# A decoder layer on one core: the product with w_out by Strassen's scheme, in seven half-size products

## The chip, the cores and the metric

One core of a Trainium2 chip. The metric is the device time of one execution in microseconds (us): the median of the runs.

## What is computed

The layer takes x (512 tokens, 1024 channels). One normalised copy of x goes through one wide input projection; two attention mixers, A and B, work on its pieces; their outputs are gated, widened to 1024 channels and merged. What matters here is the end:

```python
merged = g_m[..., :D_MODEL] * (y_a @ w_branch_a[l]) + g_m[..., D_MODEL:] * (y_b @ w_branch_b[l])
x = x + merged @ w_out[l]          # (512 x 1024) @ (1024 x 1024)
```

All of it is float32. The kernel computes each large product from three products of split operands: every float32 operand is cast to a high part (float32r) and a low part (the rest), and high times high, low times high and high times low are added up in PSUM.

## The kernel before

The whole kernel is one Python function, hybrid_kernel, that writes out five engine queues by hand. Generators for the attention (attention), the projections (gemms) and the compression (cmp) yield the cost of each piece of TensorE work; a loop at its end takes the pieces in turn and keeps a planned time. Everything that is not TensorE work is queued as a Chain: a list of steps with costs per engine, taken from a heap in order of planned time. A step with two costs (the helper either) goes to VectorE or to GpSimd, whichever the plan says ends first. So the order on each engine is fixed when the kernel is built; on the chip each engine goes through its own queue in that order and waits at semaphores.

Weights come through Stream (W): load issues a DMA of a tile (128 x 512, 256 KB) into one of four raw buffers, split casts it to the high part wh on ScalarE or GpSimd (L295, L297) and subtracts for the low part wl on VectorE or GpSimd (L299), and take hands four, two or one of them to a product. Every DMA goes through the helper dma (L212) on the SyncE queue.

The part that the change touches is the end of gemms. For each of the two mixers and each of the eight tiles j of 128 channels, gmgate makes a gate (24 matmuls of 512 columns into pgc; L1161 scales it on VectorE) and branch makes the widened mixer output (12 matmuls of 512 columns into pbr; L1179 multiplies it by the gate). With the second mixer the two are added (L1236) and the sum, 128 channels x 512 tokens, is cast to mh (L1237, ScalarE) and ml (L1238). Then comes the output product: for each of four groups of 256 output columns and each of four tiles of 128 tokens, 8 x 3 matmuls of 256 columns into a PSUM tile po, one VectorE instruction that adds 0.25 times the result to the tile xr of x (L1264), and a DMA of 128 KB to out_y. The 16 weight tiles of w_out go through the same Stream as all others; each is split once. The loads of x are issued during the last two tiles and the first columns of the output.

Of the kernel before, what the change touches and what calls it, by code (L numbers as in the profile page):

```python
# [18 lines left out]
S = 512  # L19
# [67 lines left out]
def hybrid_kernel(ctx: ExitStack, tc: tile.TileContext, x, x0, xT, wtok, wchan, gains, w1,  # L87
# [14 lines left out]
    def nm(s):  # L102
# [11 lines left out]
    ap_ = ctx.enter_context(tc.tile_pool(name="att", bufs=NATT))  # L114
    sp = ctx.enter_context(tc.tile_pool(name="sp", bufs=2))
    RES = {"g": (pg, 2), "s": (pss, 2), "t": (pst, 3), "o": (pso, 1), "sb": (sp, 3), "gmt": (sp, 3), "nraw": (sp, 4),
           "ph": (sp, 3), "P": (sp, 2), "p0": (sp, 2), "T": (sp, 2), "pf": (sp, 2)}
    held = {k: [] for k in RES}
    waiters = {k: [] for k in RES}
    owner, keep = {}, []  # L120
# [145 lines left out]
        return f  # L266


    class Stream:


        def __init__(w, tiles, bufs, hi, lo):
            w.tiles, w.bufs, w.mk_hi, w.mk_lo = tiles, bufs, hi, lo
            w.raw, w.out, w.chain, w.i, w.loaded = {}, {}, {}, 0, 0

        def load(w):
            i = w.loaded
            if i < len(w.tiles) and i - len(w.chain) < w.bufs:
                src, n = w.tiles[i]
                t = wp.tile([P, WT], F32, name=nm("wr"), tag="wraw", bufs=NRAW)[:, :n]  # L280
                w.raw[i] = t, dma(t, src, 4 * n)
                w.loaded += 1

        def split(w, upto):
            for i in range(len(w.chain), min(upto, len(w.tiles))):
                while w.loaded <= i:
                    w.load()
                n = w.tiles[i][1]
# [12 lines left out]

        def take(w, n, width):

            w.split(w.i + n)
            r = []
            for i in range(w.i, w.i + n):
                hi, lo = w.out.pop(i)
                r += [(hi[:, k:k + width], lo[:, k:k + width], w.chain[i])
                      for k in range(0, w.tiles[i][1], width)]
            w.i += n  # L310
            return r

# [160 lines left out]
    tiles = []  # L473
    for n_ in ORDER_T:
        tiles += tok_tiles(n_) if n_ in tlay else chan_tiles(n_)
    for w in range(2):
        for j in range(8):
            tiles += chan_tiles(f"gm{8 * w + j}") + [(wbr[j, w], 512)]
    for c in range(4):
        tiles += [(wout[c, i], 512) for i in range(4)]  # L480
    W = Stream(tiles, NRAW - 1, lambda: wp.tile([P, WT], F32R, name=nm("wh"), tag="whi"),
               lambda: wp.tile([P, WT], F32R, name=nm("wl"), tag="wlo"))
    W1 = Stream([(w1[kv, q], 512) for kv in range(2) for q in range(8)], 1, lambda: att("vh"), lambda: att("vl"))

    def ahead(f):

        W.split(W.i + min(4, int(f * 4 + 0.8)))

    def gemm_tok(name, emit, tags="gggg"):
        n = tlay[name][2]  # L490
# [325 lines left out]
    class Unit:  # L816
# [103 lines left out]
        def pv(u, kb):  # L920
            z, ch = u.p[kb]
            yield ch.ready
            ws = z["w"]
            if kb == 0 and u.first:
                yield room("o")
                O[0] = psum("o", "O")
            n = S - kb * P
            for i, w in enumerate(ws):
                v = u.v()[kb]
                nc.tensor.matmul(O[0][:, S - n:], v.bitcast(F32) if kb == 3 else v, w,  # L930
                                 start=(u.first and kb == 0 and i == 0), stop=(u.last and kb == 3 and not u.before))
# [265 lines left out]
    def gemms():  # L1197
# [19 lines left out]
        yield from zgate("b", 1)  # L1217
        yield from zgate("b", 2)
        yield from zgate("b", 3)
        xr = {}  # L1220
        ms = []
        for j in range(8):
            yield from gmgate(0, j)
            yield from branch(0, j)
        for j in range(8):
            yield from gmgate(1, j)
            if j == 6:
                for t in range(0, NT, 2):
                    yield room("P")
                    xp = alloc("P", "xr", (P, 1280))  # L1230
                    for i in range(2):
                        xr[t + i, 0] = xp[:, i * 512:(i + 1) * 512]
                        dma(xr[t + i, 0], x[(t + i) * P:(t + i + 1) * P, :512], 2048)
            ch = yield from branch(1, j)
            g0, g1, a, b = gms[0, j][0], gms[1, j][0], att("mh"), att("ml")
            ch.do(either(512), lambda e, g0=g0, g1=g1: e.tensor_add(g0, g0, g1))  # L1236
            ch.do({"A": ca(512)}, lambda e, g0=g0, a=a: e.copy(a, g0))  # L1237
            ch.do(either(512), lambda e, g0=g0, a=a, b=b: e.tensor_sub(b, g0, a.bitcast(F32)))  # L1238
            ms.append((a, b, ch))
        for c in range(4):  # L1240
            ws = W.take(4, 256)
            if c == 0:
                for t in range(NT):
                    xr[t, 1] = att("xr", F32)
                    dma(xr[t, 1], x[t * P:(t + 1) * P, 512:], 2048)
            st = [[(a[:, t * P:(t + 1) * P], b[:, t * P:(t + 1) * P], ch) for a, b, ch in ms] for t in range(NT)]
            pss_ = {}
            for t in range(NT):
                if c == 0 and t == 0:

                    for i in range(2):
                        yield room("g")
                        pss_[i] = psum("g", "po")
                        yield from mm3(pss_[i][:, :256], st[i][:7], ws[:7], stop=False)
                if t in pss_:
                    yield from mm3(pss_[t][:, :256], st[t][7:], ws[7:], start=False)
                    ps = pss_[t]
                else:
                    yield room("g")
                    ps = psum("g", "po")  # L1260
                    yield from mm3(ps[:, :256], st[t], ws)
                ahead((t + 1) / NT)
                xv = xr[t, c // 2][:, (c % 2) * 256:(c % 2 + 1) * 256]
                ch = Chain(now[0] + 230).do({"D": 335}, lambda e, xv=xv, ps=ps: e.scalar_tensor_tensor(  # L1264
                    xv, ps[:, :256], 0.25, xv, op0=ALU.mult, op1=ALU.add), ps)
                ch.call(lambda t=t, c=c, xv=xv: dma(out[t * P:(t + 1) * P, c * 256:(c + 1) * 256], xv, 1024))

    def cmp():
        yield from compress_h(0)
# [63 lines left out]
def _layout(inp):  # L1333
# [4 lines left out]
    for name, cols in tok_pieces().items():  # L1338
# [13 lines left out]
    wo = f["w_out"][0].reshape(4, 2, P, 4, 256).transpose(3, 0, 2, 1, 4).reshape(4, 4, P, 512)  # L1352
# [28 lines left out]
```

## Time and profile before

| | |
|---|---|
| median of 3 runs | 476.97 us (476.38 to 478.19) |
| the profiled execution | 477.26 us |
| its span, first to last instruction | 475.1 us |
| TensorE clock granted | 1.0 of full speed |
| instructions | 8579 |
| bytes moved | 49.18 MB, mean 104 GB/s |

In the rows below PE is TensorE, PEld its weight loads, DVE is VectorE, ACT ScalarE, POOL GpSimd, SP SyncE and SPq its DMA queue. A start is in us from the start of the span. A duration includes the way through the engine, so instructions of one engine that follow each other start closer together than their durations say: what counts for a queue is the distance from start to start. The time of the profiled execution is 2.16 us longer than its span, and 0.29 us over the median.

### The profile page before, as it was taken

Reading aid. Unit: us, or ns where it says so; the run is one execution under the profiler, and the core shown is the slowest. Engines: PE = TensorE matmul, PEld = TensorE weight load, DVE = VectorE, ACT = ScalarE, POOL = GpSimd, SP = SyncE. Lnnn points to the kernel's source line nnn. Section 1 sums busy time; section 2 is a strip of 40 time slices with the busy share of each in tenths; the row PEclk is TensorE's granted clock in tenths of the full one; section 3 lists DMA queues with packets and bytes.
Section 4 is the critical chain, followed back from the end, with each engine's and each line's share of the span. In section 5 each row is a group of like instructions: output and inputs, shape, how many; then the busy total and the mean of one; then the engine's idle time right before and its main releaser. Section 6 shows DMA issues by size and latency. Waiting matters only on the chain.

```text
span 475.1 us, 8579 instructions
## 1 busy us (share of the span) xinstructions
PE 467.9 (98%) x3020; PEld 421.6 (89%) x3020; DVE 336.3 (71%) x843; ACT 252.9 (53%) x603; POOL 167.5 (35%) x230
## 2 busy tenths in 40 slices
PE   9999989999999999999999999999999999999997
PEld 8999789999999989888888888888888888889997
DVE  5877999599999499977877786868734556464331
ACT  7666586588775275576776446677522222132210
POOL 0455486136663064256453324745520010000000
PEclk9999999999999999999999999999999999999999
DMA  8844244443335123032212322212122324554421
GB/s 294 243 131 112 66 112 123 144 137 117 112 110 149 52 74 105 24 88 68 67 46 66 90 90 68 66 46 67 68 66 89 111 68 118 168 187 121 140 89 46
DMA packets 27899, 49.18 MB, mean 104 GB/s; under 512 B 3088, under 2 KB 5520, under 8 KB 27856
## 3 DMA queue, kind: packets, MB, share of 16 engines
q1 hardware_dynamic: 27856, 48.63, 34.1%
q8 instruction: 24, 0.39, 0.3%
q14 instruction: 19, 0.16, 0.1%
HBM read 45.87 MB, written 2.75 MB: 102 GB/s over the span
## 4 chain that ended last, share of the span: by engine, by line
PE 87%; DVE 7%; issue 2%; ACT 2%; DMA 1%; POOL 1%; SPq 0%; DVEq 0%; POOLq 0%
PE pgc L324 28%; PE pgt L324 18%; PE po L324 10%; PE pbr L324 9%; PE O L930 6%; PE pt L896 6%; PE sps L849 3%; PE sps L850 3%; DVE wl L299 2%; PE pq L793 1%; DVE qs L801 1%; DMA x<-in_xT 1%; PE hps L687 1%; PE hps L686 1%; DVE X L658 1%
## 5 line engine op out<-in xcount | busy, mean ns | idle before, releaser
L299 DVE TENSOR_TENSOR wl<-wr,wh 128x512 fp32r<-128x512 f32 (+1 forms) x111 | 80.0, 723 | 9.1 <-ACT wh L295 8.5
L324 PE MATMUL pgc<-hh,wh 128*128 128x512 f32 x208 | 84.0, 404 | 0.0
L324 PE MATMUL pgt<-wh,hh 128*128 128x256 f32 (+1 forms) x288 | 82.6, 287 | 0.6 <-ACT nraw L552 0.6
L324 PE MATMUL pgt<-wl,hh 128*128 128x256 f32 (+1 forms) x288 | 81.6, 283 | 1.2 <-DVE wl L299 0.7
L324 PE MATMUL pgc<-hh,wl 128*128 128x512 f32 x208 | 82.1, 395 | 0.0
L324 PE MATMUL pgc<-hl,wh 128*128 128x512 f32 x208 | 82.0, 394 | 0.0
L324 PE MATMUL pgt<-wh,hl 128*128 128x256 f32 (+1 forms) x288 | 81.1, 282 | 0.0
L295 ACT CAST wh<-wr 128x512 fp32r<-128x512 f32 (+1 forms) x85 | 51.1, 615 | 23.9 <-DMA wr<-in_wout 21.5
L868 DVE CUSTOM_DVE_ANT_0 sb<-sps,T 128x512 f32<-128x512 f32 (+3 forms) x96 | 46.3, 486 | 22.9 <-PE sps L850 21.9
L883 ACT ACTIVATE P<-sb,sst 128x512 f32<-128x512 f32 (+3 forms) x88 | 50.9, 580 | 13.3 <-DVE sst L868 12.4
L887 POOL TENSOR_SCALAR P<-P,sst,gate 128x512 f32<-128x512 f32 (+3 forms) x56 | 38.5, 692 | 50.5 <-DVE sst L886 45.8
L324 PEld LDWEIGHTS pgt<-wl,hh 128*128 128x128 f32 x288 | 54.2, 188 | 1.8 <-DVE wl L299 1.1
L324 PEld LDWEIGHTS pgt<-wh,hh 128*128 128x128 f32 x288 | 54.3, 188 | 1.4 <-ACT nraw L552 0.8
L324 PEld LDWEIGHTS pgt<-wh,hl 128*128 128x128 f32 x288 | 54.3, 189 | 0.3
L297 POOL TENSOR_SCALAR wh<-wr 128x512 fp32r<-128x512 f32 (+1 forms) x39 | 25.8, 665 | 71.0 <-DMA wr<-in_wchan 48.2
L908 ACT CAST ph<-pt 128x512 fp32r<-128x512 f32 (+2 forms) x72 | 33.2, 479 | 30.1 <-PE pt L896 29.4
L324 PEld LDWEIGHTS pgc<-hl,wh 128*128 128x128 f32 x208 | 39.1, 188 | 9.1
L324 PEld LDWEIGHTS pgc<-hh,wh 128*128 128x128 f32 x208 | 39.2, 188 | 7.4
L324 PEld LDWEIGHTS pgc<-hh,wl 128*128 128x128 f32 x208 | 39.2, 188 | 7.2
L365 POOL TENSOR_TENSOR nr<-nss,mhalf 128x4 f32<-128x4 f32 x28 | 30.8, 1102 | 33.6 <-DVE nss L364 26.9
L896 PE MATMUL pt<-cst,P 128*128 128x128 f32 x232 | 40.6, 272 | 0.6 <-POOL P L887 0.6
L910 DVE TENSOR_TENSOR pl<-pt,ph 128x512 fp32r<-128x512 f32 (+2 forms) x72 | 38.2, 549 | 3.2 <-ACT ph L908 3.2
(202 smaller groups left out, 1062.4 us busy)
## 6 DMA issues: line engine op xcount, KB each, us to landing
wr<-in_wchan SPq DMA_DIRECT2D x52, 256.0 KB, 2.7
wr<-in_wtok SPq DMA_DIRECT2D x36, 256.0 KB, 2.8
T<-rtab SPq DMA_DIRECT2D x16, 256.0 KB, 3.8
wr<-in_w SPq DMA_DIRECT2D x16, 256.0 KB, 2.7
wr<-in_wbr SPq DMA_DIRECT2D x16, 256.0 KB, 2.6
wr<-in_wout SPq DMA_DIRECT2D x16, 256.0 KB, 3.1
xr<-in_x SPq DMA_DIRECT2D x8, 256.0 KB, 3.9
out_y<-xr SPq DMA_DIRECT2D x16, 128.0 KB, 1.7
```

The lines of the kernel that those rows point to most:

```text
L295: e.copy(hi, raw)
L297: e.tensor_scalar(hi, raw, 1.0, 1.0, op0=ALU.mult, op1=ALU.mult)
L299: c.do(either(n), lambda e, hi=hi, lo=lo, raw=raw: e.tensor_sub(lo, raw, hi.bitcast(F32))).mark((w, 1, i))
L324: nc.tensor.matmul(dst, sts[i][a], mvs[i][b], start=(start and i == a == b == 0), stop=(stop and i == n - 1 and b == 1))
L365: c.do({"p": 430 + 150 * w}, lambda e: e.tensor_tensor(v(dst), v(ss), mhalf[:parts, :w], op=ALU.pow))
L868: e.tensor_tensor_reduce(z["sb"][:, :L], sps[:, :L], T[:, S - L:], scale=-1.0, scalar=3e38, op0=ALU.add, op1=ALU.min, accum_out=st[:, 0, b ...
L883: e.activation(pv(), z["sb"][:, :L], AF.Exp, bias=st[:, 0, b:b + 1], scale=-1.0, accum_out=st[:, 1, b:b + 1])
L887: c.do({"P": 315 + 0.834 * L}, lambda e: e.tensor_scalar(pv(), pv(), st[:, 2, b:b + 1], g, op0=ALU.mult, op1=ALU.mult))
L896: nc.tensor.transpose(pt[:, (b - kb) * P:(b - kb + 1) * P], u.p0 if u.p0 is not None and b == 0 else u.pb[:, POFF[b] + kb * P:POFF[b] + (k ...
L908: e.copy(z["w"][0], pt[:, :w])
L910: ch.do({"D": cd(w)}, lambda e: e.tensor_sub(z["w"][1], pt[:, :w], z["w"][0].bitcast(F32)), pt)
L930: nc.tensor.matmul(O[0][:, S - n:], v.bitcast(F32) if kb == 3 else v, w, start=(u.first and kb == 0 and i == 0), stop=(u.last and kb == 3 ...
```

## The change

The output product is cut into blocks: A is the merged input, A11 its tokens 0 to 255 in channels 0 to 511, A12 the same tokens in channels 512 to 1023, A21 and A22 the other tokens; B is w_out cut in the same way. Seven products of 256 x 512 by 512 x 512 take the place of eight:

| product | left factor | right factor | goes to |
|---|---|---|---|
| 1 | A11 | B11 | all four blocks of the output |
| 2 | A12 | B21 | block 11 |
| 3 | S4 = A12 - S2 | B22 | block 12 |
| 4 | A22 | B21 - T2 | block 21 |
| 5 | S1 = A21 + A22 | T1 = B12 - B11 | blocks 12 and 22 |
| 6 | S2 = S1 - A11 | T2 = B22 - T1 | blocks 12, 21 and 22 |
| 7 | S3 = A11 - A21 | B22 - B12 | blocks 21 and 22 |

Each product is 2 tiles of tokens x 4 tiles of channels x 3 matmuls of 512 columns; the last tile of product 4 is made in two halves of 256 columns. A tile leaves PSUM when it is done. Products 1 and 7 are moved up: product 1 stands between gmgate and branch of the second mixer's tile 4, product 7 between those of its tile 6 (EARLY). Products 5 and 6 come first after tile 7, in two passes (three tiles of channels of both, then the fourth), and then 2, 3 and 4.

The left factors are made in merged by VectorE or GpSimd from the merged tiles and split like before. The right factors are objects of the class Sum: their sources are loaded by load_sums in 36 DMAs of 256 KB (B11 twice, B12 twice, B22 three times, B21 twice, 4 tiles each) in place of 16, into the pool ph, which held the transposed attention weights; it has six buffers now, and the low parts pl of those come from it too. VectorE or GpSimd subtracts where two sources make a factor. The four tiles of T1 and T2 are kept in wsum. Where product 1 leaves PSUM, ScalarE copies it times 0.25 to a tile u, VectorE adds it to one output tile, and GpSimd adds u to three others.

```diff
+EARLY = {4: 1, 6: 7}
+PACE = 800
...
-           "ph": (sp, 3), "P": (sp, 2), "p0": (sp, 2), "T": (sp, 2), "pf": (sp, 2)}
+           "ph": (sp, 6), "P": (sp, 2), "p0": (sp, 2), "T": (sp, 2), "pf": (sp, 2)}
...
+    (b11, b12), (b21, b22) = [[[wout[i, j, k] for k in range(4)] for j in range(2)] for i in range(2)]
+    t1 = [Sum(z, k, True, None, True) for k, z in enumerate(zip(b12, b11))]
+    t2 = [Sum((b22[k],), k, True, t1[k]) for k in range(4)]
+    right = {1: [Sum((z,), home=True) for z in b11], 7: [Sum(z) for z in zip(b22, b12)], 5: t1, 6: t2, 2: [Sum((z,)) for z in b21],
+             3: [Sum((z,)) for z in b22], 4: [Sum((b21[k],), k, False, t2[k]) for k in range(4)]}
...
         for j in range(8):
             yield from gmgate(1, j)
-            if j == 6:
+            if j == 0:
...
+                W.load_sums()
...
+            if j == 2:
...
+                for t, c in ((0, 0), (1, 0), (2, 0), (3, 0), (2, 1), (3, 1), (0, 1), (1, 1)):
+                    dma(xr[t, c], x[t * P:(t + 1) * P, c * 512:(c + 1) * 512], 2048)
+            if j in EARLY:
+                yield from early[EARLY[j]]()
             ch = yield from branch(1, j)
...
+        if j < 4:
+            q = att("ms", F32)
+            sub(c, q[:, lo_], m[:, lo_], m[:, hi_])
+            part(c, a[:, lo_], b[:, lo_], m[:, lo_])
+            part(c, a[:, hi_], b[:, hi_], q[:, lo_])
...
+        c.do(either(256), lambda e: e.tensor_add(q[:, hi_], n[:, hi_], m[:, hi_]))
+        c.call(lambda: d.start(c.t))
+        sub(c, n[:, lo_], q[:, hi_], n[:, lo_])
+        sub(c, n[:, hi_], m[:, lo_], n[:, lo_])
+        c.call(lambda: f.start(c.t))
+        part(d, u, v, q[:, hi_])
+        part(c, x, y, n)
+        part(f, a, b, m)
...
+            u = att("u", F32)
+            z[1].do({"A": 478}, lambda e: e.activation(u, z[0], AF.Copy, scale=0.25))
+            add(z, t, 0, 0, True)
+            for r, col in ((1, 0), (1, 1), (0, 1)):
+                add(z, t, r, col, src=u)
...
+        yield from products((S1, "tt", five), (S2, "ss", six))
+        for left, tags, r, col in ((A12, "gg", 0, 0), (S4, "to", 0, 1), (A22, "sst", 1, 0)):
```

The order of all engines is the same as before up to the second mixer's tile 0. Two places behind it matter below. The first is VectorE around the second mixer's tiles 5 to 7. Before, a tile j is the scaling of the gate (L1161), two or three low parts of weights (wl, L299), the product with pbr (L1179), the sum (L1236) and its low part (L1238); the rows begin behind the scaling of tile 6:

```order
L299 TENSOR_TENSOR wl_5585<-wr_5537,wh_5584 128x512
L299 TENSOR_TENSOR wl_5592<-wr_5544,wh_5591 128x512
L1179 SCALAR_TENSOR_TENSOR gm_5531<-gm_5531,pbr_5575 128x512
L299 TENSOR_TENSOR wl_5599<-wr_5550,wh_5598 128x512
L1236 TENSOR_TENSOR gm_4981<-gm_4981,gm_5531 128x512
L1238 TENSOR_TENSOR ml_5601<-gm_4981,mh_5600 128x512
L1161 TENSOR_TENSOR gm_5602<-pgc_5603,R 128x512
```

Now (wq and wl of L348 are the sources and low parts of product 7's right factor, ms, s1l, sl and ml parts of the left factors, gm_5681 the gate of tile 6):

```order
L348 TENSOR_TENSOR wl_5670<-wq_5195,wh_5669 128x512
L1341 TENSOR_TENSOR gm_4719<-gm_4719,gm_5608 128x512
L1359 TENSOR_TENSOR sl_5607<-gm_3831,sh_5606 128x512
L348 TENSOR_TENSOR wl_5676<-wq_5265,wh_5675 128x512
L1378 TENSOR_TENSOR ms_5314<-gm_3961,gm_4719 128x256
L1355 TENSOR_TENSOR gm_3961<-ms_5314,gm_3961 128x256
L1359 TENSOR_TENSOR s1l_5605<-ms_5314,s1h_5604 128x256
L1355 TENSOR_TENSOR gm_3961<-gm_4719,gm_3961 128x256
L1250 TENSOR_TENSOR gm_5681<-pgc_5682,R 128x512
L348 TENSOR_TENSOR wl_5728<-wq_5328,wh_5727 128x512
L348 TENSOR_TENSOR wl_5726<-wq_5307,wh_5725 128x512
```

The low parts of product 7's third and fourth weight tile (wl_5726, wl_5728) stand behind the scaling of tile 6's gate, which needs the whole of pgc_5682; on TensorE the matmuls of product 7 follow pgc_5682 at once.

The second place is SyncE's queue of DMAs. Before, the loads for the second mixer's tiles 5 to 7 are these, three to a tile:

```order
L212 DMA wr_5407<-in_wchan 128x512
L212 DMA wr_5414<-in_wbr 128x512
L212 DMA wr_5420<-in_wchan 128x512
L212 DMA wr_5472<-in_wchan 128x512
L212 DMA wr_5479<-in_wbr 128x512
L212 DMA wr_5485<-in_wchan 128x512
```

Now, ahead of wr_5422, the second weight tile of the gate of tile 4:

```order
L214 DMA wr_5345<-in_wchan 128x512
L214 DMA wq_5351<-in_wout 128x512
L214 DMA wq_5360<-in_wout 128x512
L214 DMA xr_5363<-in_x 128x512 x2
L214 DMA xr_5364<-in_x 128x512 x2
L214 DMA xr_5367<-in_x 128x512
L214 DMA xr_5368<-in_x 128x512
L214 DMA xr_5365<-in_x 128x512
L214 DMA xr_5366<-in_x 128x512
L214 DMA wq_5403<-in_wout 128x512
L214 DMA wr_5422<-in_wchan 128x512
L214 DMA wr_5427<-in_wbr 128x512
```

All eight loads of x and three of w_out now stand between two loads of gate weights that used to follow each other; six more loads (four wq from in_wout and two wr) stand just ahead of the first of these rows.

## Rows read from the trace of the kernel before

**Rows 1.** The page's busy time of each engine over the span, and its 40 slices of the span (busy tenths; PEclk is the granted clock in tenths).

```profile
PE 467.9 (98%) x3020; PEld 421.6 (89%) x3020; DVE 336.3 (71%) x843; ACT 252.9 (53%) x603; POOL 167.5 (35%) x230
...
PE   9999989999999999999999999999999999999997
...
DVE  5877999599999499977877786868734556464331
...
POOL 0455486136663064256453324745520010000000
PEclk9999999999999999999999999999999999999999
```

**Rows 2.** The chain that ended last, in order of time, from the second mixer's tile 0 to the end: start, us, what, count. A piece of TensorE work begins here where the one before it ended.

```profile
359.30 5.55 PE pgc L324 x24
364.86 2.80 PE pbr L324 x12
...
392.73 5.54 PE pgc L324 x24
398.27 2.79 PE pbr L324 x12
...
423.33 2.78 PE pbr L324 x12
426.10 5.37 PE po L324 x45
431.48 0.02 issue
431.50 0.44 DVE xr L1264
431.94 0.04 issue
431.98 40.01 PE po L324 x336
471.99 0.02 issue
472.01 0.42 DVE xr L1264
```

**Rows 3.** Busy time of each engine in stretches: one tile of the second mixer (gate and branch) and two stretches of the output product. Columns: stretch, its length, then PE, PEld, DVE, ACT, POOL busy us (instructions), granted clock, DMA share, GB/s.

```profile
401.06:409.39 8.33, 8.33 (x38) 6.77 (x37) 4.57 (x7) 2.28 (x4) 0.62 (x1) 1.00 0.30 91
...
437.50:448.90 11.40, 11.40 (x99) 11.40 (x98) 4.09 (x8) 2.48 (x4) 0.00 (x0) 1.00 0.48 144
448.90:460.40 11.50, 11.50 (x100) 11.50 (x99) 4.09 (x8) 1.86 (x3) 0.00 (x0) 1.00 0.35 109
```

**Rows 4.** VectorE in order of time in the second mixer's tile 0, and at the first output tiles: start, us, instruction, and in brackets how long the engine stood idle before it and for whom.

```profile
364.89 0.69 DVE L1161 TENSOR_TENSOR gm<-pgc,R 128x512 f32<-128x512 f32 x1 [4.26 <-PE pgc L324]
...
367.69 0.69 DVE L1179 SCALAR_TENSOR_TENSOR gm<-gm,pbr 128x512 f32<-128x512 f32 x1 [0.20 <-PE pbr L324]
368.29 0.68 DVE L299 TENSOR_TENSOR wl<-wr,wh 128x512 fp32r<-128x512 f32 x1
368.89 0.68 DVE L1236 TENSOR_TENSOR gm<-gm,gm 128x512 f32<-128x512 f32 x1
370.27 0.69 DVE L1238 TENSOR_TENSOR ml<-gm,mh 128x512 fp32r<-128x512 f32 x1 [0.69 <-ACT mh L1237]
...
431.50 0.77 DVE L1264 SCALAR_TENSOR_TENSOR xr<-po,xr 128x256 f32<-128x256 f32 x2 [2.08 <-PE po L324]
```

**Rows 5.** GpSimd's groups of instructions over the span, shapes kept apart: count, busy us, mean ns of one, idle time before.

```profile
L297 POOL TENSOR_SCALAR wh<-wr 128x512 fp32r<-128x512 f32 x38 | 25.2, 665 | 71.0 <-DMA wr<-in_wchan 48.2 <-DMA wr<-in_wout 11.0 <-DMA wr<-in_wtok 6.3
L299 POOL TENSOR_TENSOR wl<-wr,wh 128x512 fp32r<-128x512 f32 x13 | 18.2, 1398 | 24.1 <-ACT wh L295 23.4
...
L564 POOL TENSOR_TENSOR nxn<-nraw,nr 128x256 f32<-128x256 f32 x6 | 4.0, 668 | 0.3
```

**Rows 6.** VectorE and GpSimd side by side, in order of time, at two moments (sps and O are PSUM tiles, wr and wh lie in SBUF).

```profile
54.67 1.31 POOL L299 TENSOR_TENSOR wl<-wr,wh 128x512 fp32r<-128x512 f32 x1
54.91 1.62 DVE L299 TENSOR_TENSOR wl<-wr,wh 128x512 fp32r<-128x512 f32 x1
...
203.57 1.29 POOL L299 TENSOR_TENSOR wl<-wr,wh 128x512 fp32r<-128x512 f32 x1
203.74 0.69 DVE L868 CUSTOM_DVE_ANT_0 sb<-sps,T 128x512 f32<-128x512 f32 x1 [1.33 <-PE sps L850]
204.36 0.68 DVE L959 TENSOR_TENSOR ys<-O,ot 64x512 f32<-64x512 f32 x1
```

**Rows 7.** The same view as rows 3, for three stretches in which the DMA queue was full; the last column is what it moved.

```profile
5.00:10.00 5.00, 4.88 (x35) 4.33 (x36) 4.06 (x7) 4.54 (x9) 0.62 (x1) 1.00 1.01 376
10.00:15.00 5.00, 5.00 (x44) 5.00 (x44) 5.00 (x9) 4.99 (x10) 1.31 (x1) 1.00 1.06 337
...
412.00:414.00 2.00, 2.00 (x10) 1.61 (x9) 0.69 (x1) 0.00 (x0) 0.00 (x0) 1.00 0.88 237
```

**Rows 8.** The end, in order of time: the last matmul, the last VectorE instruction and the issue of the last DMA.

```profile
471.70 0.28 PE L324 MATMUL po<-wl,mh 128*128 128x256 f32 x1
472.01 0.42 DVE L1264 SCALAR_TENSOR_TENSOR xr<-po,xr 128x256 f32<-128x256 f32 x1 [2.40 <-PE po L324]
472.47 0.33 SPq L212 DMA_DIRECT2D out_y<-xr  x1
```

More of the change, by code (lines that the diff above doesn't have):

```diff
@@ L266, in all_of, with __init__, dst, fire @@
         return f
+    class Sum:
+        def __init__(z, srcs, keep=None, put=False, prior=None, home=False):
+            z.srcs, z.keep, z.put, z.prior, z.home = srcs, keep, put, prior, home
+            z.raw, z.t, z.c, z.left, z.next = [], 0.0, Chain(held=True), 1, None
+            if prior:
+                z.left += 1
+                prior.next = z
+            if len(srcs) == 2:
+                z.c.do(either(512), lambda e: e.tensor_sub(z.dst(), z.raw[0], z.raw[1]), lambda: z.raw[1])
+            elif keep is not None:
+                z.c.do(either(512), lambda e: e.tensor_sub(z.dst(), z.raw[0], wsum[keep]))
+            if put:
+                z.c.call(lambda: release(z.raw[0], z.c.t))
+        def dst(z):
+            return wsum[z.keep] if z.put else z.raw[0]
+        def fire(z, t):
+            z.t = max(z.t, t)
+            z.left -= 1
+            if not z.left:
+                z.c.start(max(now[0], z.t))
+        def end(z):
+            if not z.put:
+                release(z.raw[0], z.c.t)
+            if z.next:
+                z.next.fire(z.c.t)
+    wsum = []
     class Stream:
@@ L273, in __init__ @@
             w.tiles, w.bufs, w.mk_hi, w.mk_lo = tiles, bufs, hi, lo
-            w.raw, w.out, w.chain, w.i, w.loaded = {}, {}, {}, 0, 0
+            w.raw, w.out, w.chain, w.i, w.loaded, w.ahead, w.next = {}, {}, {}, 0, 0, 0, 0
         def load(w):
+            while w.loaded < len(w.tiles) and isinstance(w.tiles[w.loaded], Sum):
+                w.loaded += 1
             i = w.loaded
-            if i < len(w.tiles) and i - len(w.chain) < w.bufs:
+            if i < len(w.tiles) and w.ahead < w.bufs:
                 src, n = w.tiles[i]
@@ L308, in take @@
                 r += [(hi[:, k:k + width], lo[:, k:k + width], w.chain[i])
-                      for k in range(0, w.tiles[i][1], width)]
+                      for k in range(0, hi.shape[-1], width)]
             w.i += n
@@ L485, in ahead @@
     def ahead(f):
-        W.split(W.i + min(4, int(f * 4 + 0.8)))
+        n, k = 0, min(4, int(f * 4 + 0.8))
+        while k and W.i + n < len(tiles):
+            k -= not getattr(tiles[W.i + n], "home", False)
+            n += 1
+        W.split(W.i + n)
     def gemm_tok(name, emit, tags="gggg"):
@@ L1232, in gemms @@
                         xr[t + i, 0] = xp[:, i * 512:(i + 1) * 512]
[L1233 removed]
+                for t in range(NT):
+                    tag = "sb" if t < 2 else "T"
+                    yield room(tag)
+                    xr[t, 1] = alloc(tag, "xr")
+                for t, c in ((0, 0), (1, 0), (2, 0), (3, 0), (2, 1), (3, 1), (0, 1), (1, 1)):
+                    dma(xr[t, c], x[t * P:(t + 1) * P, c * 512:(c + 1) * 512], 2048)
@@ L1240, in gemms @@
[L1240 to L1266, printed above, removed]
@@ new lines, in hybrid_kernel, with products @@
+    one = []
+    xr = {}
+    pend = {}
+    def products(*todo):
+        ws = [W.take(4, 512) for _ in todo]
+        ps, n = {}, 0
+        m = 3 if len(todo) > 1 else 4
+        for k in (0, 3) if m == 3 else (0,):
+            e = 4 if k else m
+            for i, (left, tags, f) in enumerate(todo):
+                for t, tag in enumerate(tags):
+                    o = slice((t - 1) * 256, t * 256) if t and len(tags) > 2 else slice(0, 512)
+                    t = min(t, 1)
+                    st = [(a[:, t * P:(t + 1) * P], b[:, t * P:(t + 1) * P], c) for a, b, c in left[k:e]]
+                    if not k:
+                        yield room(tag)
+                        ps[i, t, o.start] = psum(tag, "po")
+                    p = ps[i, t, o.start]
+                    for v in mm3(p[:, o], st, [(h[:, o], l[:, o], c) for h, l, c in ws[i][k:e]], start=not k, stop=e == 4):
+                        yield v
+                        if not callable(v):
+                            n += 1
+                            ahead(n / 8 / len(todo))
+                    if e == 4:
+                        f(t, (p, Chain(now[0] + 230)), o)
@@ new lines, in add @@
+    def add(z, t, r, col, frees=False, o=slice(0, 512), src=None):
+        p, c = z
+        key = 2 * r + t, col
+        dst = xr[key]
+        pend[key] = pend.get(key, 0) + 1
+        if src is None:
+            c.do({"D": cd(o.stop - o.start)}, lambda e: e.scalar_tensor_tensor(
+                dst[:, o], p[:, o], 0.25, dst[:, o], op0=ALU.mult, op1=ALU.add), p if frees else None)
+        else:
+            c.do({"P": cg(512)}, lambda e: e.tensor_add(dst, dst, src))
+        c.call(lambda: pend.__setitem__(key, pend[key] - 1))
@@ new lines, in send, with f, out1 @@
+    def send(z, t, r, col, o=slice(0, 512)):
+        key = 2 * r + t, col
+        def f():
+            assert pend[key] == (o.stop < 512 and not z[2:])
+            dma(out[key[0] * P:(key[0] + 1) * P, col * 512 + o.start:col * 512 + o.stop], xr[key][:, o],
+                4 * (o.stop - o.start))
+        z[1].call(f)
+    def out1():
+        def f(t, z, _):
+            u = att("u", F32)
[3 more added lines that the diff above has]
+                add(z, t, r, col, src=u)
+        yield from products((A11, "tt", f))
@@ new lines, in out7, with f, output, five @@
+    def out7():
+        def f(t, z, _):
+            add(z, t, 1, 0)
+            add(z, t, 1, 1, True)
+        yield from products((S3, "ss", f))
+        i = tiles.index(right[5][0])
+        for k in range(4):
+            Chain(now[0] + PACE * k).call(lambda k=k: W.split_sum(i + k))
+    early = {1: out1, 7: out7}
+    def output():
+        def five(t, z, _):
+            add(z, t, 1, 1)
+            add(z, t, 0, 1, True)
+        def six(t, z, _):
+            add(z, t, 1, 1)
+            send(z, t, 1, 1)
+            add(z, t, 0, 1)
+            add(z, t, 1, 0, True)
+        yield from products((S1, "tt", five), (S2, "ss", six))
+        for left, tags, r, col in ((A12, "gg", 0, 0), (S4, "to", 0, 1), (A22, "sst", 1, 0)):
+            def f(t, z, o):
+                for q in (slice(0, 256), slice(256, 512)):
+                    if o.start <= q.start < o.stop:
+                        y = z if o.stop - o.start > 256 else (*z, 1)
+                        add(z, t, r, col, q.stop == o.stop, q)
+                        send(y, t, r, col, q)
+            yield from products((left, tags, f))
```

98 lines of the change are left out of this document (85 added, 13 removed).

## The prediction, made before the changed kernel ran

> **What bounds the kernel now.** I read the busy times and slices first: TensorE is busy 98% of the span at the full clock in every slice, VectorE 71%, and in the last tenth VectorE is half idle and GpSimd idle altogether [rows 1]. Next the chain that ended last: from 359.30 to 471.99 it is matmuls end to end, apart from one turn of VectorE at 431.50, and the output product takes 426.10 to 471.99, 45.89 us [rows 2]. So what counts is how many matmuls this stretch has, how long each takes, and whether their inputs stay ahead. Then the stretches: a tile of the second mixer leaves VectorE 4.57 us busy of 8.33 and GpSimd 0.62; the output product leaves VectorE 4.09 of 11.4 and GpSimd nothing [rows 3]. The change spends that idle time. The end is one VectorE turn and one DMA after the last matmul [rows 8].
>
> **TensorE, the gain.** Before: 384 matmuls of 256 columns; 336 of them took 40.01 us, 0.119 each [rows 2]. A matmul of 512 columns: from 359.30 to 426.10 there are 8 tiles of 36, 288 matmuls in 66.80 us, 0.232 each [rows 2]. The change issues 7 x 24 = 168 matmuls of 512 columns, but 12 of them as 24 halves: 156 x 0.232 = 36.2 and 24 x 0.119 = 2.9, together 39.0, and 0.16 for the last matmul's way out (0.28 against 0.12 from start to start [rows 8]): 39.2. That is 6.7 less than 45.89. The widths alone give little (two of 256 against one of 512 is 0.238 to 0.232); the eighth product gives the rest.
>
> **The end.** The last piece is again 256 columns wide, read by one VectorE instruction and sent as 128 KB, as at 472.01 and 472.47 [rows 8]: no difference. Moving products 1 and 7 up costs TensorE nothing in itself, as one accumulator follows another without a gap today [rows 2].
>
> **VectorE and GpSimd, the price.** VectorE has 55 instructions more, GpSimd 18. A 512-wide VectorE instruction starts 0.60 after the one before it, a 256-wide one takes 0.35 (0.77 for two, less the way out) [rows 4]. On GpSimd a 512-wide copy takes 0.62 to 0.67, a two-input instruction 1.3 alone (mean 1.4), a 256-wide one 0.67 [rows 5, 6]. The two also get in each other's way: a VectorE subtraction that began 0.24 after GpSimd's took 1.62 in place of 0.68 and ended 0.55 after GpSimd's end, while two VectorE instructions that read PSUM kept 0.69 and 0.68 beside the same kind of GpSimd work [rows 6]. So VectorE's SBUF-to-SBUF work and GpSimd's work add up, and the reading of PSUM lies beside.
>
> The place where this binds first is product 7. Without stalls the gate of tile 4 ends at 398.27 [rows 2], product 1 at 403.84, its first half at 401.05, branch 4 at 406.62, the gate and branch of tile 5 at 412.19 and 414.97, the gate of tile 6 at 420.53, and there product 7 begins. Its third weight tile's low part is read by the ninth matmul, issued at 420.53 + 8 x 0.232 - 0.16 = 422.2. VectorE makes that low part (wl_5726) as the 26th instruction counted from the first read of product 1, and only two behind the scaling of tile 6's gate, which can't start before 420.53 + 0.03 (364.86 to 364.89 [rows 2, 4]).
>
> - From below: three starts of 0.60 from 420.56, and 0.08 for the way out, is 422.44. Product 7 waits 0.2 at least, however idle VectorE was before.
> - From above: of the 26, 19 are wide and 7 narrow, 13.9 us. GpSimd has in the same stretch the six additions of u (7.8), a narrow subtraction (0.7) and three copies (1.9), 10.4. If nothing lay beside anything, 24.3 in the 21.2 us from 401.05: 3.1 late.
> - In between: six of the 26 read PSUM and may lie beside, 3.6 us; that leaves 20.7 in 21.2, full but not over. VectorE also goes in order and stands when a low part waits for its high part on ScalarE, 0.69 each time now [rows 4], and there is a narrow pair of that kind in the stretch for each of tiles 4 and 5.
>
> I take 0.2 and one such wait, 0.9, rounded to 1.0: nearer the lower end, because the sum without the PSUM reads fits.
>
> [...]
>
> The next place is product 6, whose last left factor (sl of tile 7) comes from branch 7's result. The merged tile 7 is complete at 437.23; 42 matmuls of products 5 and 6 go before the first that reads its S2, at 437.23 + 42 x 0.232 = 447.0. From 401.05 that is 45.9 us for 66 VectorE instructions, 52 wide and 14 narrow, 36.1, and 13.7 of GpSimd's (the 10.4, and in the rest one wide and one narrow subtraction and two copies, 3.3). All in a row 49.8, 3.9 late; with the 13 PSUM reads (7.8) beside, 42.0, 3.9 early. A delay at product 7 gives this place as much more time, so the two don't add. I cost it at nothing; its cover is those 4 us.
>
> Products 2, 3 and 4 find VectorE lighter: in 16.7 us of matmuls two or three low parts and two narrow reads each. Nothing.
>
> **DMA.** 36 loads of w_out in place of 16 are 20 x 262 KB = 5.2 MB more. Today a tile of the second mixer moves 91 GB/s at a DMA share of 0.30 [rows 3]. The tight place is SyncE's queue: from the first free raw buffer to the second weight tile of the gate of tile 4, 19 loads (5.0 MB) stand in one row. The buffers come free with the low parts of product 1's weights, behind tile 1's gate (359.30 + 8.35 + 5.57 = 373.2, and two VectorE turns: 374.7). The tile is wanted at 392.73 + 12 x 0.232 = 395.5, less 1.2 for cast and subtraction: 394.3. That is 19.6 us, or 254 GB/s. Full queues in this trace moved 376 and 337 GB/s, and one that was paced by its issues 237 [rows 7]. I take the full ones: this queue is issued ahead, so nothing is late.
>
> **The sum.** 477.26 (profiled execution) - 6.7 + 1.0 = 471.6. The profiled execution is 0.29 over the median, so the median should be **471.3**.
>
> **The rivals.**
>
> 1. *VectorE and GpSimd become the bound between product 1 and product 6.* For it: both upper sums above, and the block of 1.62 [rows 6]. Against: PSUM reads kept their time there. The cost is 2.2 to 4.0: 472.5 to 474.3, and a little beyond if VectorE's waits for ScalarE come on top.
> 2. *The DMA queue is late for the gate of tile 4, and the kernel is slower.* 5.0 MB wanted in 19.6 us. At 237 GB/s [rows 7] they take 21.0, 1.4 late; at 200, 24.9, 5.3 late, 475.6. From 173 GB/s down (28.8 us, 9.2 late) the loss exceeds the gain by more than 2.4 and the time is 479.5 or more. For it: one queue in order, where a load that waits for its buffer holds the gate weights behind it, and the eight loads of x ahead. Against: 337 and 376 when the queue is full [rows 7].
> 3. *No stall beyond the 0.2, or none.* VectorE comes to product 7 on time: 470.2 to 470.5. For it: the 20.7 in 21.2. That the matmuls of 512 columns don't keep 0.232 with operands of the new kind would be the only way for the gain itself to fail; 288 in a row speak against it [rows 2].
>
> **How the numbers follow.** Forecast (stall 0.3 to 2.2, 470.5 to 472.5) 0.62; rival 1 0.18, of which 0.02 lies beyond 474.6; rival 2 0.12, of which 0.05 slower than 479.4; rival 3 0.08. About 0.5% (2.4 us) is what a measurement of this kernel can tell from no change. Faster by more than that, below 474.6: 0.62 + 0.16 + 0.08 = 0.86. Within: 0.02 + 0.07 = 0.09. Slower: 0.05. The range of 8 in 10 runs from rival 3's lower end less the spread of runs, 470.0, to rival 1's upper end, 474.6; out of it are rival 2 (0.12), 0.02 of rival 1 and about 0.03 below.
>
> **What would show it.** Right: 180 po matmuls, the full ones 0.232 from start to start; the chain end to end in TensorE from tile 0 to the end but for one wait at product 7 for a wl of L348, of 0.2 to 2; VectorE over 90% busy from product 1 to product 6; subtractions of 1 to 1.8 us beside L1431 on GpSimd; the last matmul about 5.7 earlier, near 466. Wrong: TensorE waiting at the gate of tile 4 or 5 for a wr (rival 2); several waits for sl or s1l in products 5 and 6, or more than 2.2 in all (rival 1); matmuls of po over 0.24 from start to start.

## The result: 1.3% faster, and the profile after

The changed kernel takes **471.04 us** (median of 4 runs, 470.95 to 471.85); the kernel before, run beside it, 477.32 (476.38 to 478.19). The ratio is 0.9873, with a 95% interval of 0.985 to 0.9895. The profiled execution is 471.12 us, its span 469.3.

Busy times and slices of the changed kernel, to be held against [rows 1]:

```profile
PE 461.2 (98%) x2816; PEld 408.4 (87%) x2816; DVE 373.2 (80%) x900; ACT 263.5 (56%) x628; POOL 195.5 (42%) x248
...
DVE  5877999599999589988787686867862697799994
...
POOL 0264486046655054355554314637521140752160
PEclk9999999999999999999999999999999999999999
```

TensorE has 204 matmuls fewer (2816 against 3020), the same full clock (0.999 of full speed in the mean, 1.000 before), and the same 98%: it still sets the time. VectorE's last tenth went from 4, 3, 3, 1 to 9, 9, 9, 4 and GpSimd's from nothing to 2, 1, 6, 0: the idle time has been spent.

The chain that ended last, from the second mixer's tile 0 on, to be held against [rows 2] (start, us, what, count):

```profile
359.33 5.55 PE pgc L397 x24
...
398.29 5.48 PE po L397 x24
...
415.03 0.69 DVE gm L1268
...
421.18 0.60 DVE gm L1250
421.78 0.24 DVE wl L348
...
422.30 0.70 DVE wl L348
...
423.04 3.98 PE po L397 x16
...
438.20 27.84 PE po L397 x132
...
466.07 0.42 DVE xr L1428
```

Two things are to be seen. Product 1 stands in one piece of 24 at 398.29, and from 438.20 on there are 132 matmuls without a gap. Between them the chain leaves TensorE once, from the end of tile 5's branch (414.94) to the last 16 matmuls of product 7. It runs over VectorE there, almost without a gap, and ends with the scaling of a gate (gm, L1250) and, behind it, two low parts of weights (wl, L348). The last VectorE turn begins at 466.07 in place of 472.01, 5.94 earlier.

That one place in order of time, TensorE's matmuls of product 7 (start, us, instruction, idle time before):

```profile
421.99 0.40 PE L397 MATMUL po<-wh,ml 128*128 128x512 f32 x1
423.04 0.50 PE L397 MATMUL po<-wl,mh 128*128 128x512 f32 x1 [0.65 <-DVE wl L348]
423.38 0.39 PE L397 MATMUL po<-wh,mh 128*128 128x512 f32 x1
```

The record calls this 0.65 idle, but the matmul lost more, since each one's tail of 0.40 overlaps the next: from start to start it is 1.05 in place of 0.23, and the matmul after it follows at 0.34 in place of 0.23. The wait costs 0.82 + 0.11 = **0.93**.

Busy time of each engine in stretches from the middle of product 1 to the middle of products 5 and 6, to be held against [rows 3] (columns as there); product 7 lies in the third:

```profile
401.06:409.39 8.33, 8.33 (x37) 6.78 (x37) 7.38 (x8) 2.73 (x5) 7.13 (x5) 1.00 0.42 144
409.39:420.50 11.11, 11.11 (x49) 8.97 (x48) 10.71 (x16) 3.12 (x7) 7.64 (x7) 1.00 0.34 116
420.50:431.00 10.50, 9.85 (x43) 7.68 (x42) 10.50 (x19) 5.71 (x11) 2.18 (x1) 1.00 0.30 95
431.00:441.00 10.00, 10.00 (x44) 8.10 (x44) 10.00 (x17) 4.68 (x9) 2.46 (x3) 1.00 0.33 105
441.00:451.00 10.00, 10.00 (x45) 8.12 (x44) 9.14 (x18) 4.78 (x9) 2.87 (x2) 1.00 0.35 107
```

VectorE, 4.57 of 8.33 us busy before in the first of them, is 89 to 100% busy in every one, and GpSimd 7.13 where it was 0.62. Yet TensorE is short only in the third, by 0.65.

VectorE and GpSimd beside each other after product 1, to be held against [rows 6]:

```profile
402.26 10.13 POOL L1431 TENSOR_TENSOR xr<-xr,u 128x512 f32<-128x512 f32 x6 [15.73 <-ACT u L1446]
402.62 0.68 DVE L1428 SCALAR_TENSOR_TENSOR xr<-po,xr 128x512 f32<-128x512 f32 x1
...
406.64 1.18 DVE L282 TENSOR_TENSOR ws<-wq,wq 128x512 f32<-128x512 f32 x1
407.75 0.67 DVE L1268 SCALAR_TENSOR_TENSOR gm<-gm,pbr 128x512 f32<-128x512 f32 x1
...
409.45 1.78 DVE L1341 TENSOR_TENSOR gm<-gm,gm 128x512 f32<-128x512 f32 x1
```

Subtractions from SBUF to SBUF take 1.18 to 1.78 beside GpSimd's additions in place of 0.68; instructions that read PSUM (xr, and the gm of L1268) keep 0.68. GpSimd's six additions take 10.13, 1.69 each, where one alone took 1.3.

The end, to be held against [rows 8]:

```profile
465.75 0.28 PE L397 MATMUL po<-wl,mh 128*128 128x256 f32 x1
466.07 0.42 DVE L1428 SCALAR_TENSOR_TENSOR xr<-po,xr 128x256 f32<-128x256 f32 x1 [0.99 <-PE po L397]
466.52 0.33 SPq L214 DMA_DIRECT2D out_y<-xr  x1
```

It is the same three steps, and from the VectorE turn to the end of the span 3.2 us against 3.1.

### The profile page after: what moved, and what is told of

The parts are those of the page before. It is cut to its first block, busy times and chain, and to the rows that moved or that the text cites. A ratio compares the mean times of both kernels' runs of the same rounds, so it can differ in the third digit from the quotient of the medians.

```text
span 469.3 us, 8293 instructions
## 1 busy us (share of the span) xinstructions
PE 461.2 (98%) x2816; PEld 408.4 (87%) x2816; DVE 373.2 (80%) x900; ACT 263.5 (56%) x628; POOL 195.5 (42%) x248
## 4 chain that ended last, share of the span: by engine, by line
PE 85%; DVE 8%; ACT 3%; issue 1%; DMA 1%; POOL 1%; SPq 0%; DVEq 0%; POOLq 0%
PE pgc L397 27%; PE pgt L397 18%; PE pbr L397 10%; PE po L397 8%; PE O L1017 6%; PE pt L982 6%; PE sps L935 3%; PE sps L936 3%; DVE wl L372 1%; PE pq L879 1%; DVE qs L887 1%; DMA x<-in_xT 1%; ACT hh L462 1%; PE hps L773 1%; PE hps L772 1%
## 5 line engine op out<-in xcount | busy, mean ns | idle before, releaser
L372 DVE TENSOR_TENSOR wl<-wr,wh 128x512 fp32r<-128x512 f32 (+1 forms) x93 | 71.3, 772 | 5.5 <-ACT wh L368 4.8
L969 ACT ACTIVATE P<-sb,sst 128x512 f32<-128x512 f32 (+3 forms) x88 | 50.9, 580 | 13.3 <-DVE sst L954 12.5
L368 ACT CAST wh<-wr 128x512 fp32r<-128x512 f32 (+1 forms) x75 | 45.3, 616 | 7.1 <-DMA wr<-in_wbr 2.5
L397 PEld LDWEIGHTS pgc<-hh,wh 128*128 128x128 f32 x208 | 39.2, 189 | 7.3
L397 PEld LDWEIGHTS pgc<-hh,wl 128*128 128x128 f32 x208 | 39.2, 189 | 7.2
L973 POOL TENSOR_SCALAR P<-P,sst 128x512 f32<-128x512 f32 (+3 forms) x32 | 20.8, 652 | 37.8 <-DVE sst L972 35.9
```

The source lines that it names most:

```text
L397: nc.tensor.matmul(dst, sts[i][a], mvs[i][b], start=(start and i == a == b == 0), stop=(stop and i == n - 1 and b == 1))
L969: e.activation(pv(), z["sb"][:, :L], AF.Exp, bias=st[:, 0, b:b + 1], scale=-1.0, accum_out=st[:, 1, b:b + 1])
L973: c.do({"P": 315 + 0.834 * L}, lambda e: e.tensor_scalar(pv(), pv(), st[:, 2, b:b + 1], g, op0=ALU.mult, op1=ALU.mult))
```

## The experiments

### Where the gain is from: a seventh less work, or wider matmuls?

The kernel before with an output product 512 columns wide, all eight products of it, and the last tile in two halves:

```diff
-        for c in range(4):
-            ws = W.take(4, 256)
+        for c in range(2):
+            ws = W.take(8, 512)
```

> The kernel before, with eight half-size products' worth of work as it was, but the output made in two groups of 512 columns (192 matmuls of 512 columns, the last tile in two halves) and no Strassen sums. Theory 1 (the seventh part less of TensorE's work is the gain): 180 x 0.232 + 24 x 0.119 = 44.6 us against 45.9, 1.3 less at best; the eight weight tiles of the first group are wanted within 5.6 us, for which VectorE needs 4.8, so a wait of 0 to 1 eats most of it: 476 to 477.3, not to be told from the kernel before. Theory 2 (the gain comes from wider matmuls, which halve the weight loads that fill TensorE's load path in the output stage): about as the changed kernel, 471 to 472.

Measured: 477.73 us against 477.72 for the kernel before on the same chip; the ratio is 1.0004 (0.9995 to 1.0013). By the rows, 168 wide and 48 narrow matmuls are 168 x 0.232 + 48 x 0.119 = 44.7, only 1.0 under 384 x 0.119 = 45.7, and two waits took that back, as the waits of TensorE from 425 on show:

```profile
PE po L324 <- DVE wl L299: 0.7, 1, 0.7
PE po L324 <- ACT wh L295: 0.2, 1, 0.2
```

In this form width alone gives nothing that can be measured, and without the waits it could give 1.0 at most. The counterpart is the changed kernel with product 1 computed twice into the same accumulator, the first pass overwritten:

```diff
+                    if left is A11:
+                        yield from mm3(p[:, o], st, ms_, start=not k, stop=e == 4)
                     for v in mm3(p[:, o], st, ms_, start=not k, stop=e == 4):
```

> The changed kernel with the 24 matmuls of product 1 issued twice into the same PSUM tiles (the second pass starts anew). Theory 1 (TensorE's count of matmuls sets the time): 24 x 0.232 = 5.57 more, less up to 0.45 because VectorE gets that time to catch up before product 7: span 474.4 to 474.9. Theory 3 (VectorE sets the pace from product 1 to product 6): most of the 5.57 is hidden behind VectorE, span 470 to 472.

Measured: span 474.5, 5.2 more than the 469.3, with one wait of TensorE from tile 0 to the end, for a wl of L348 again (0.4). 24 matmuls are 24 x 0.232 = 5.57. The run stood 0.21 earlier already where product 1 begins (398.08 against 398.29), which is most of the difference: from there to the last VectorE turn it is 73.19 against 67.78, 5.41 more. VectorE did not catch up as expected: from start to start the wait costs 0.9 again. So the gain is the count of matmuls, nearly one for one.

### Who makes the wait at product 7: GpSimd's additions

Two kernels take GpSimd's additions of product 1 away, in two ways. If product 7 waits because subtractions took 1.18 to 1.78 beside those additions in place of 0.68, its wait of 0.65 should shrink without them. In the first, VectorE adds product 1 to all four blocks out of PSUM; there is no copy u and no addition on GpSimd:

```diff
-            u = att("u", F32)
-            z[1].do({"A": 478}, lambda e: e.activation(u, z[0], AF.Copy, scale=0.25))
-            add(z, t, 0, 0, True)
-            for r, col in ((1, 0), (1, 1), (0, 1)):
-                add(z, t, r, col, src=u)
+            for r, col in ((0, 0), (1, 0), (1, 1), (0, 1)):
+                add(z, t, r, col, (r, col) == (0, 1))
```

> The changed kernel, but product 1 is added to all four output blocks by VectorE straight from PSUM, 8 instructions; the copy u on ScalarE and the six additions on GpSimd are gone. VectorE has 3.6 us more of its own work between product 1 and product 7. [...] Theory 3 (VectorE's own work is the bound, whoever shares it): the wait grows by up to 3.6, span 470 to 473.

Measured: 470.80 us, ratio 0.9859 (0.9842 to 0.9875), span 469.0; the wait fell to 0.2. VectorE in order of time, at the place where its subtractions took 1.18 to 1.78 in the changed kernel:

```profile
405.02 0.68 DVE L372 TENSOR_TENSOR wl<-wr,wh 128x512 fp32r<-128x512 f32 x1
```

Every subtraction there, L1341's too, is back at 0.68. But the planner moved other work in this kernel too (the low part that TensorE waits for is now GpSimd's), so the second one keeps every instruction on its engine in its order and only makes the six additions short: 8 of their 512 columns, so that the rest of three output blocks lacks product 1.

```diff
-            c.do({"P": cg(512)}, lambda e: e.tensor_add(dst, dst, src))
+            c.do({"P": cg(512)}, lambda e: e.tensor_add(dst[:, :8], dst[:, :8], src[:, :8]))
```

> The changed kernel with the six additions of u on GpSimd (L1431) made on the first 8 columns alone, so that the rest of those three output blocks lacks product 1. The order of instructions on every engine is that of the changed kernel, and VectorE's and TensorE's work is the same to the instruction. [...] Theory 3 (VectorE's own work makes it late, GpSimd only runs beside it): the wait stays 0.65, span 469.3, and the subtractions keep their lengths.

Measured: 470.82 us, ratio 0.9863 (0.9846 to 0.9879), span 468.9. GpSimd, VectorE and TensorE in order of time:

```profile
404.51 0.67 POOL L1431 TENSOR_TENSOR xr<-xr,u 128x8 f32<-128x8 f32 x4 [1.85 <-ACT u L1446]
...
407.82 0.68 DVE L1341 TENSOR_TENSOR gm<-gm,gm 128x512 f32<-128x512 f32 x1
...
410.44 1.78 POOL L346 TENSOR_SCALAR wh<-wq 128x512 fp32r<-128x512 f32 x3
...
412.21 0.69 DVE L1250 TENSOR_TENSOR gm<-pgc,R 128x512 f32<-128x512 f32 x1 [2.35 <-PE pgc L397]
...
415.06 0.69 DVE L1268 SCALAR_TENSOR_TENSOR gm<-gm,pbr 128x512 f32<-128x512 f32 x1 [1.56 <-PE pbr L397]
...
416.27 0.69 DVE L348 TENSOR_TENSOR wl<-wq,wh 128x512 fp32r<-128x512 f32 x1
...
420.66 0.69 DVE L1250 TENSOR_TENSOR gm<-pgc,R 128x512 f32<-128x512 f32 x1
...
422.02 0.40 PE L397 MATMUL po<-wh,ml 128*128 128x512 f32 x1
422.60 0.50 PE L397 MATMUL po<-wl,mh 128*128 128x512 f32 x1 [0.18 <-DVE wl L348]
422.94 0.39 PE L397 MATMUL po<-wh,mh 128*128 128x512 f32 x1
```

VectorE now stands idle for 2.35 and 1.56, waiting for TensorE, and scales tile 6's gate at 420.66 in place of 421.10. GpSimd and VectorE of the changed kernel in the same stretch:

```profile
414.14 2.71 POOL L346 TENSOR_SCALAR wh<-wq 128x512 fp32r<-128x512 f32 x3
...
415.03 0.69 DVE L1268 SCALAR_TENSOR_TENSOR gm<-gm,pbr 128x512 f32<-128x512 f32 x1 [0.26 <-PE pbr L397]
...
416.29 1.09 DVE L348 TENSOR_TENSOR wl<-wq,wh 128x512 fp32r<-128x512 f32 x1
...
421.10 0.68 DVE L1250 TENSOR_TENSOR gm<-pgc,R 128x512 f32<-128x512 f32 x1
```

So the additions reach product 7 by a detour. They held VectorE up for some 4 us (from L282 at 402.01 to s1l at 413.14 are 11.13; in the kernel with 8 columns, from 401.54 to 409.44, 7.90, of which 1.15 idle), but at 415.03 the changed kernel's VectorE, too, stood idle for TensorE, 0.26 for tile 5's branch: by then it had made up all of that. What is left is that GpSimd's next work came later. Its three casts (wh, L346), over at 412.22 in the kernel with 8 columns, now run from 414.14 to 416.85. The low part that VectorE begins beside them, at 416.29, takes 1.09 in place of 0.69 and ends 0.53 after them, much like the one in [rows 6]. The next instruction starts 1.02 after it in place of 0.60: this 0.42 is nearly the whole 0.44 by which the scaling comes later.

The wait that is left in the kernel with 8 columns is, but for 0.1 by which VectorE is still late, the one that its order forces: 0.35 from start to start and 0.11 for the matmul behind it, 0.46 in place of 0.93. So the additions cost TensorE 0.4 to 0.5. In time the three kernels can't be told apart (spans 469.3, 469.0, 468.9); the rows tell them apart.

### Does the early place of product 7 pay?

Product 7 stands in tile 6's slot. A first kernel moved it to tile 7's by the table alone:

```diff
-EARLY = {4: 1, 6: 7}
+EARLY = {4: 1, 7: 7}
```

> The changed kernel with product 7 between the gate and the branch of tile 7 in place of tile 6 (EARLY = {4: 1, 7: 7}). Theory A (an early product only has to wait for its own inputs): VectorE has 8.4 us more for product 7's weights, its wait goes, span 468.7. Theory B (product 7 also sets when T1 and T2 are split, since those splits are queued behind it and need its weight buffers): only the 2.8 us of branch 7 are left for 4 splits of T1, 4 subtractions and 4 splits of T2, some 12 VectorE instructions of 0.6 beside the left factors; products 5 and 6 wait 4 to 5 us in all, span 473 to 474.

Measured: span 475.7, more than either theory said, with waits of 3.5 in all for wl and wh in the products. This says little. The longest of the waits was 1.6, and the mean granted clock of the run is 0.992, where the mended kernel below has 1.000: its last 127 matmuls, from 443.50 on, took 28.89, 2.1 more than 103 x 0.232 + 24 x 0.119 = 26.75. And the move also made the weights' sums for product 5 be split a second time, at another moment and from other values, so that product 5 isn't the same there and four splits are added. The mended kernel splits them once:

```diff
-            Chain(now[0] + PACE * k).call(lambda k=k: W.split_sum(i + k))
+            Chain(now[0] + PACE * k).call(lambda k=k: i + k in W.chain or W.split_sum(i + k))
```

> As p7late, product 7 between the gate and the branch of tile 7, but each tile of T1 is split once (in p7late the start by hand and the stream's own start both split it, and the second took values of T2). Theory A (an early product only has to wait for its own inputs): wait gone, span 468.7. Theory B (the splits of T1 and T2 are queued behind product 7, with 2.8 us of matmuls left for them): products 5 and 6 wait 2.5 to 4 in all, span 471.3 to 473.

Measured: span 472.2, 2.9 more, as theory B said. Its engines in two stretches of products 5 and 6:

```profile
440.00:445.00 5.00, 4.45 (x19) 3.07 (x18) 5.00 (x7) 2.83 (x6) 1.65 (x1) 1.00 0.49 157
445.00:450.00 5.00, 3.49 (x14) 2.30 (x14) 4.93 (x11) 2.47 (x5) 0.00 (x0) 1.00 0.40 107
```

TensorE is short by 0.55 and 1.51, waiting for the last left factors of product 5 (s1h, s1l) and a wl, while VectorE is full (9.93 of 10, against 9.14 from 441 to 451 in the changed kernel). The run stood 0.36 later already where product 1 begins (398.65 against 398.29), ahead of the move: the early place is worth some 2.5, in one run.

### The DMA queue's margin

The eight loads of x stand in SyncE's queue ahead of the weights of tile 4's gate. Here each is issued twice, 2.1 MB more:

```diff
-                for t, c in ((0, 0), (1, 0), (2, 0), (3, 0), (2, 1), (3, 1), (0, 1), (1, 1)):
+                for t, c in 2 * ((0, 0), (1, 0), (2, 0), (3, 0), (2, 1), (3, 1), (0, 1), (1, 1)):
```

> The changed kernel with its eight loads of x issued twice in a row, 2.1 MB more in SyncE's queue ahead of the second weight tile of the gate of tile 4. In the changed kernel that tile's cast waited for its DMA until 393.5 and its low part was done at 394.8, 0.6 to 0.8 before TensorE reads it. Theory M (the queue was full from 380 to 393 and the gate of tile 4 had under 1 us to spare): 2.1 MB at 340 to 400 GB/s are 5.2 to 6.2 us, less 0.7, so TensorE waits 4.5 to 5.5 at the gate of tile 4, span 473.8 to 474.8. Theory N (the loads of the gates are ahead by more than that, as with 4 us for the kernel before): no wait at the gate, span 469.3 to 470.

Measured: span 477.6, 8.3 more than 469.3. The place was expected, the size was not. Its TensorE in order of time at tile 4's gate, and the stretches from there (columns as in [rows 3]; the third from last is the granted clock):

```profile
400.19 0.80 PE L397 MATMUL pgc<-hh,wh 128*128 128x512 f32 x1 [4.31 <-ACT wh L368]
...
402.36 0.63 PE L397 MATMUL pgc<-hh,wl 128*128 128x512 f32 x1
402.79 0.63 PE L397 MATMUL pgc<-hl,wh 128*128 128x512 f32 x1
```

```profile
400.00:402.00 2.00, 1.81 (x4) 1.19 (x5) 1.83 (x3) 1.37 (x3) 0.00 (x0) 0.50 0.70 183
402.00:404.00 2.00, 2.00 (x6) 1.60 (x5) 0.85 (x2) 0.00 (x0) 0.00 (x0) 0.50 1.06 378
404.00:406.00 2.00, 2.00 (x6) 1.56 (x5) 0.00 (x0) 0.00 (x0) 0.00 (x0) 0.50 0.84 245
```

The granted clock, 1.00 up to 399 and 0.81 from 399 to 400, is 0.50 from 400 to 406: matmuls follow each other at 0.43 in place of 0.23, and 12 of them took 5.79, where 12 of a branch take 2.78. So the wait cost 4.3, the lower clock 3.0, and the 14 matmuls of product 1 that follow some 0.3 more (3.52 for 14 x 0.232 = 3.25); the wait at product 7 (0.9 in the record, 0.7 before) and a start 0.4 later, ahead of the wait, make up the rest.

How near the changed kernel itself is to this, its DMA in a stretch before, and ScalarE and VectorE in order of time at the same weight tile:

```profile
390.00:392.00 2.00, 2.00 (x10) 1.62 (x9) 0.67 (x1) 0.63 (x1) 0.00 (x0) 1.00 1.06 407
```

```profile
393.47 1.90 ACT L368 CAST wh<-wr 128x512 fp32r<-128x512 f32 x3 [2.13 <-DMA wr<-in_wchan]
394.12 0.69 DVE L372 TENSOR_TENSOR wl<-wr,wh 128x512 fp32r<-128x512 f32 x1 [0.63 <-ACT wh L368]
```

ScalarE stood 2.13 for the load, the low part was done at 394.81, and TensorE reads it near 395.6: 0.7 to 0.8 us to spare.

### The last tile in two halves

The last tile of product 4 whole, read by two VectorE instructions and sent in two pieces at the end:

```diff
-(A22, "sst", 1, 0)
+(A22, "ss", 1, 0)
```

> The changed kernel with the last tile of product 4 made whole, 12 matmuls of 512 columns in place of 24 of 256. TensorE ends 0.08 earlier (24 x 0.119 against 12 x 0.232), but then two VectorE instructions of 256 columns and two DMAs come behind the last matmul in place of one: 0.35 for the VectorE turn and about as much for the second issue, of which the larger counts. Span 469.5 to 469.8. If the halves were worth nothing: 469.2.

Measured: span 470.2, 0.9 more, above the range expected. Its last VectorE turn:

```profile
466.35 0.76 DVE L1428 SCALAR_TENSOR_TENSOR xr<-po,xr 128x256 f32<-128x256 f32 x2 [2.02 <-PE po L397]
```

Of this, 0.34 is not the edit's: the run stood that much later already at 438.54, where the last stretch of matmuls begins. These took 0.05 less (27.79 against 27.84), and from the VectorE turn to the end it is 3.85 against 3.23: the halves are worth 0.6 less 0.05, in one run.

## Why the prediction was right, point by point

The sum was 471.6 for the profiled execution, which took 471.12. Term by term:

| Step | Predicted | Measured | From |
|---|---|---|---|
| Output product without its wait | 39.2 | 38.9 | 5.48 + (6.49 - 0.93) + 27.84 |
| Wait at product 7 | 1.0 | 0.93 | start to start |
| The eight tiles of the second mixer | 66.8 | 66.9 | 359.33 to 438.20, less products 1 and 7 |
| Last VectorE turn to the end of the span | no difference | +0.1 | 3.23 against 3.1 |
| Outside the span | no difference | -0.3 | 471.12 - 469.3 against 477.26 - 475.1 |

(Product 7 ran from the end of tile 6's gate, 414.94 + 5.57 = 420.51, to 427.02, some 6.49.)

- **TensorE.** Right: 0.232 for a wide matmul with the new operands too, 132 in a row at 27.84 for 108 x 0.232 + 24 x 0.119 = 27.9. Two experiments give the cause: width alone 1.0004, one product back +5.2 of span, 5.4 from that product on.
- **The wait.** Right in place, buffer and size, but its two parts were cut wrongly. The forced part was put at 0.2 and is 0.46: VectorE's second low part was done at 422.55 even with GpSimd's additions out of the way (421.26 + 1.29 in the kernel with 8 columns), 0.11 after the 422.44 of the sum, and the restart, which the sum left out, cost another 0.11 at the matmul behind. The other part was taken as one VectorE wait for ScalarE of 0.69; between 402 and 423 no wait of VectorE for ScalarE is recorded. It is GpSimd's: its casts, put off by the additions, lengthen one subtraction of VectorE (1.09 for 0.69), and the scaling comes at 421.10 in place of 420.66, so 0.4 to 0.5. That two wrongly cut parts came to 0.9 and the runs to 0.93 is in part luck.
- **VectorE and GpSimd.** Right that subtractions take 1 to 1.8 beside L1431 (1.18 to 1.78) and that PSUM reads keep their time (0.67 to 0.68). VectorE was over 90% busy in all stretches but the first (89%). This is what the first rival rested on. It cost little because the sum over the whole stretch was not the one that counted. VectorE read product 1 at 402.62 and not at 401.05, having stood 2.40 for a load of w_out, and still was idle for TensorE at 415.03. What product 7 waited for is the unbroken row of work from there to 422.99. (By the traces VectorE has 57 instructions more, 900 against 843, and not 55; nothing hangs on it.)
- **Product 6.** Right at nothing, but the cover of 3.9 was too large. The factor in question, in order of time on VectorE and at its first reader:

```profile
445.67 0.68 DVE L1359 TENSOR_TENSOR sl<-gm,sh 128x512 fp32r<-128x512 f32 x1
...
447.94 0.40 PE L397 MATMUL po<-wh,sl 128*128 128x512 f32 x1
```

  It was done at 446.35 and read at 447.94: 1.6 to spare, with TensorE already 0.93 late. What took the rest wasn't tried. Moving product 7 back by one tile used this margin up.
- **DMA.** Right that nothing TensorE reads was late, but it was close. At the 337 to 376 GB/s that the sum took, 5.0 MB need 13.3 to 14.8 of the 19.6 us, which leaves 5 to 6; 0.7 to 0.8 was left, so part of this was luck. Once full, the queue did move 407 GB/s, but from 374.7 to 380 it moved 201 and from 382 to 393.5 319. What held it wasn't tried. The second rival was priced too low: it counted the lateness alone, and here TensorE's clock added 3.0 to a wait of 4.3. A wait of 4.3 already took more than the whole gain: a span of 477.6 against the 475.1 before.

## What to carry to other kernels

Where TensorE is busy to the end, count matmuls, not columns: in this case 24 matmuls more, 5.57 by the count, cost 5.4, and wider ones gave a ratio of 1.0004. Before spending another engine's idle time, sum VectorE's and GpSimd's SBUF work as if they were one engine (here a subtraction took 1.18 to 1.78 beside GpSimd's additions and 0.68 without them), leave out what reads PSUM (0.67 to 0.68 beside them too), and look at the first place where TensorE wants a result of it. Count from the last moment before that place at which the engine stands idle (here 415.03, after 0.26 of it), since what it lost earlier is made up there; what another engine was put off to do may still come beside it. A wait of TensorE cost more here than its idle record (0.93 for 0.65): the matmul behind it also started late, at 0.34 in place of 0.23, and with a wait of 4.31 the granted clock fell to 0.50.

## What the runs showed of the hardware that was not expected

- While TensorE stood for 4.31 us, the granted clock fell (0.81 from 399 to 400); it was 0.50 from 400 to 406, and 12 matmuls took 5.79 in place of 2.78. With the wait of 0.65 the stretch's clock stayed 1.00. With product 7 in tile 7's slot the first kernel, its longest wait 1.6, had a mean granted clock of 0.992 over the span, the mended one, its longest 0.9, 1.000.
- A short wait shown as 0.65 cost 0.93 from start to start, one shown as 0.18 cost 0.46.
- GpSimd slowed too: six additions beside VectorE took 1.69 each, where a two-input instruction alone took 1.3. In the kernel with 8 columns four took 0.67 together. Three of its casts took 2.71 beside VectorE's subtractions and 1.78 while VectorE stood idle.
- The DMA moved 407 GB/s in a stretch of 2 us, above the 376 of [rows 7].
